# A feed-forward block by seven products: two more blocks of this form, one weight sum moved into an accumulating DMA, and another way to merge two streams of work

## The chip, the cores and the metric

The kernel runs on one core of a Trainium2 chip. The metric is the device time of one execution in microseconds (us). TensorE (PE) multiplies, VectorE (DVE) and ScalarE (ACT) do elementwise work, GpSimd (POOL) does little here but issue some transfers, SyncE (SP) issues the other transfers from HBM.

## The reference

Two decoder layers over 256 tokens of width 2048, all in float32. Each layer projects the normed input, runs a spatial gating unit beside windowed attention, projects back, and then runs the feed-forward part, which is where the change lies:

```
h2 = rms_norm(x, norm2_g[l])
x = x + (jax.nn.silu(h2 @ w_gate[l]) * (h2 @ w_up[l])) @ w_down[l]
```

`w_gate` and `w_up` are 2048 x 5632, `w_down` is 5632 x 2048. The inner width of 5632 is cut into 11 blocks of 512 columns, numbered 0 to 10.

## The kernel before

**Three matmuls for one.** Every float32 weight tile is split into a rounded high part `wh` (ScalarE, L95) and the remainder `wl` (VectorE, L96). A product is then three matmuls into the same PSUM bank: high x high, high x low, low x high (`mm3`, L124 to L127). A loaded raw tile holds 2 x 512 columns per partition (512 KB). A *standard unit* (`unit`, L129) loads one such tile, splits it and issues 12 matmuls (two row blocks, two token tiles). The raw tiles have a ring of 6 buffers, `wh` and `wl` rings of 4 each.

**Two forms of a feed-forward block.** In the standard form (`gate_up`, L651) a block takes 8 units for the gate and 8 for the up projection. In the other form (`seven`, L568) the two token tiles and the two halves of the inner dimension make a 2 x 2 by 2 x 2 block product over gate and up together, computed by seven products in the manner of Strassen and Winograd in place of eight. This needs sums of activations (made once per layer) and four sums of weight tiles per step, done by VectorE:

```
t1 = b11 + b12                     (L594)
t2 = t1 + b22                      (L595)
b12 = b12 + b22                    (L596)
kept[i] = t2 of step i, + b21      (L621, in the second half)
```

Each product is an `s_unit` (L571): split one tile, issue 6 matmuls. A block has a first half of 4 steps with 4 products each (banks m0 to m3), an evacuation of the four banks (L605 to L612), a second half of 4 steps with 3 products each (banks n0 to n2, L615 to L625), and a second evacuation with the gate (L626 to L632). So a block takes 28 products of 6 matmuls. `t1` takes a raw buffer; the four `t2` of a block live from the first half into the second in a ring of four.

**Down projection.** `down` (L665) takes two blocks at a time: for each of four column blocks it runs two units per block and adds the result to the residual (L680). It cannot start before the activations of its blocks are transposed (`act_T`, L556, some two to three units of work after the block's end, into the eight-deep ring `aT`). While they are missing, it yields False.

**Two streams.** `s_stream` (L638) runs the blocks of `S_BLOCKS` in the seven-product form. `std_stream` (L686) runs `STD_ORDER`: the remaining blocks in standard form and all down projections. The loop at L693 to L702 merges them: `s_stream` yields 0.5 after each product and "turn" at each evacuation, and the loop takes standard units according to what is owed: `STD_SHARE` (1.42) per 1.0, raised to at least 2 at a turn, in a `while`. What is still owed while down yields False stays owed. Standard units left at the end run behind the last block. The framework places instructions on each engine by its own priorities, so the order on an engine follows this program order only roughly.

Of the kernel before, what the change touches and what calls it, by code (L numbers as in the profile page):

```python
# [16 lines left out]
ALU = mybir.AluOpType  # L17
# [22 lines left out]
NI = 3584 // NB  # L40
NFF = DFF // NB
ND = D // NB
S_BLOCKS = (1, 3, 5, 7, 8, 9, 10)
STD_ORDER = (
    ("gu", 0), ("gu", 2), ("down", (0, 1)), ("gu", 4), ("down", (2, 3)), ("gu", 6),
    ("down", (4, 5)), ("down", (6, 7)), ("down", (8, 9)), ("down", (10,)),
)
STD_SHARE = 1.42
RL = 512
WARM = 12  # L50

# [12 lines left out]
def trunk(ctx, tc, x, xt, w_in, w_out, w_gate, w_up, w_down, sgu_w, sgu_g, consts,  # L64
          rel_bias, onehot, radd, out):
    nc = tc.nc
# [15 lines left out]
    def raw_load(src, parts=1):  # L82
        raw = wp.tile([P, 2, NB], F32, tag="raw", name="raw", bufs=6)
        n = 2 // parts
        for i in range(parts):
            nc.sync.dma_start(raw[:, i * n : (i + 1) * n, :], src[:, i * n : (i + 1) * n, :])
        return raw

    def split2(raw):
        wh = wp.tile([P, 2, NB], F32R, tag="wh", name="wh", bufs=4)  # L90
        wl = wp.tile([P, 2, NB], F32R, tag="wl", name="wl", bufs=4)
        step = 2 if clock[0] > 1 else 1
        for j in range(0, 2, step):
            src = raw[:, j : j + step, :]
            nc.scalar.copy(wh[:, j : j + step, :], src)  # L95
            nc.vector.tensor_tensor(  # L96
                wl[:, j : j + step, :], src, f(wh[:, j : j + step, :]), ALU.subtract
            )
        return wh, wl
# [8 lines left out]
    def tick(w=1.0):  # L108
        clock[0] += w
        due = sorted((e for e in pending if e[0] <= clock[0]), key=lambda e: e[:2])  # L110
        pending[:] = [e for e in pending if e[0] > clock[0]]
        for e in due:
            e[2]()
# [10 lines left out]
    def mm3(acc, ah, al, wh, wl, first, last):  # L124
        nc.tensor.matmul(acc, ah, wh, start=first, stop=False)  # L125
        nc.tensor.matmul(acc, ah, wl, start=False, stop=False)  # L126
        nc.tensor.matmul(acc, al, wh, start=False, stop=last)  # L127
# [128 lines left out]
    for lay in range(L):  # L256
# [307 lines left out]
        def act_later(b, sg, act_T=act_T):  # L564
            for c in range(2):
                later(2 + c, lambda c=c: act_T(b, c, sg))

        def seven(b, lay=lay, pairs2=pairs2, ext2=ext2, act_later=act_later):  # L568
            bank = [pa.tile([P, NB], F32, tag="acc", name=f"m{i}") for i in range(4)]

            def s_unit(raw, m, i, op, first, last):  # L571
                wh, wl = split2(raw)
                for j in range(2):
                    ah, al = (op(2 * i + j, h) for h in range(2))
                    mm3(bank[m], ah, al, wh[:, j, :], wl[:, j, :], first and j == 0, last and j == 1)
                tick(0.5)

            def a_op(k, t):
                return lambda p, h: pairs2[p][:, h, k, t * P : (t + 1) * P]

            def e_op(n):
                return lambda p, h: ext2[p][:, h, n, :]

            kept = []
            for i in range(4):
                b12 = raw_load(w_up[lay, b, i, 0])
                b11 = raw_load(w_gate[lay, b, i, 0])
                b22 = raw_load(w_up[lay, b, i, 1])
                t1 = wp.tile([P, 2, NB], F32, tag="raw", name="t1", bufs=6)
                t2 = ap.tile([P, 2, NB], F32, tag="spt", name="t2", bufs=4)  # L590
                first, last = i == 0, i == 3
                s_unit(b11, 0, i, a_op(0, 0), first, last)
                yield 0.5
                nc.vector.tensor_tensor(t1, b11, b12, ALU.add)  # L594
                nc.vector.tensor_tensor(t2, t1, b22, ALU.add)  # L595
                nc.vector.tensor_tensor(b12, b12, b22, ALU.add)  # L596
                s_unit(t1, 1, i, e_op(1), first, last)
                yield 0.5
                s_unit(t2, 3, i, e_op(2), first, last)
                yield 0.5  # L600
                s_unit(b12, 2, i, e_op(0), first, last)
                yield 0.5
                kept.append(t2)
            m1 = zp.tile([P, NB], F32, tag="z", name="m1")
            nc.scalar.copy(m1, bank[0])  # L605
            u1 = zp.tile([P, NB], F32, tag="z", name="u1")
            nc.vector.tensor_tensor(u1, bank[3], m1, ALU.add)
            c22 = zp.tile([P, NB], F32, tag="z", name="c22")
            c21 = zp.tile([P, NB], F32, tag="z", name="c21")
            nc.vector.tensor_tensor(c21, bank[2], u1, ALU.add)  # L610
            nc.vector.tensor_tensor(c22, bank[1], c21, ALU.add)
            nc.vector.tensor_tensor(u1, bank[1], u1, ALU.add)  # L612
            yield "turn"
            bank = [pa.tile([P, NB], F32, tag="acc", name=f"n{i}") for i in range(3)]
            for i in range(4):  # L615
                b21 = raw_load(w_gate[lay, b, i, 1])
                b22 = raw_load(w_up[lay, b, i, 1])
                first, last = i == 0, i == 3
                s_unit(b21, 0, i, a_op(1, 0), first, last)
                yield 0.5  # L620
                nc.vector.tensor_tensor(kept[i], kept[i], b21, ALU.add)  # L621
                s_unit(kept[i], 1, i, a_op(1, 1), first, last)
                yield 0.5
                s_unit(b22, 2, i, e_op(3), first, last)
                yield 0.5  # L625
            sg = [m1, c21]  # L626
            for t, m in ((0, m1), (1, c21)):
                nc.vector.tensor_tensor(m, bank[t], m, ALU.add)
                nc.scalar.activation(m, m, AF.Silu, scale=rstd2[t])
            nc.vector.tensor_tensor(u1, bank[2], u1, ALU.add)  # L630
            for t, c in ((0, u1), (1, c22)):
                nc.vector.scalar_tensor_tensor(sg[t], c, nrstd2[t], sg[t], ALU.mult, ALU.mult)  # L632
            act_later(b, sg)
            yield "turn"
# [3 lines left out]
        def s_stream(seven=seven):  # L638
            for b in S_BLOCKS:
                yield from seven(b)  # L640
# [45 lines left out]
        def std_stream(gate_up=gate_up, down=down):  # L686
            for k, (kind, what) in enumerate(STD_ORDER):
                if kind == "gu":
                    yield from gate_up(what)
                else:  # L690
                    yield from down(what, k == len(STD_ORDER) - 1)

        other = std_stream()  # L693
        owed = 0.0
        for said in s_stream():
            owed = max(owed, 2.0) if said == "turn" else owed + said * STD_SHARE
            while owed >= 1.0 and next(other, False):
                owed -= 1.0
        seven_done[0] = True
        for went in other:  # L700
            if not went:
# [89 lines left out]
```

## Time and profile before

| | |
|---|---|
| runs, median (range) | 2025.38 us (2020.27 to 2030.16) |
| the profiled execution, its own time | 2025.57 us |
| its span, first to last instruction | 2023.9 us |
| TensorE busy | 1984.0 us, 8990 instructions |
| VectorE busy | 1666.0 us, 1925 instructions |
| ScalarE busy | 1132.3 us, 1415 instructions |
| GpSimd busy | 67.5 us, 65 instructions |
| loads on SP's queue | 407.01 MB |

A row of a group of instructions gives its line, engine, operation, result and sources by the program's names, shapes and count; then busy time in us and the mean duration of one in ns; then the time in which its engine was idle just before, and what ended most of that. Matmul rows overlap: a matmul's row is longer than the distance to the next one's start. A timeline row gives start, duration, engine, line, operation, and in brackets the idle time before it with its releaser.

### The profile page before, as it was taken

To read this page: it belongs to the slowest core of one execution; us is meant where nothing else is said; L and a number is where in the kernel's file an instruction comes from. 1 tells how busy PE (TensorE), PEld (TensorE's weight loads), DVE (VectorE), ACT (ScalarE), POOL (GpSimd) and SP (SyncE) were. 2 spreads that over 40 slices of the span, in tenths; PEclk is the share of its full clock that TensorE was granted. 3 is DMA by queue.
4 is the path that set the end of the run, shared out by engine and by line. 5 is a ranking of instruction groups with operands and counts; after the bars stand their busy time and mean duration, and the time that the engine had idled before them with its cause. 6 is when DMAs were issued, how large, how long until landed. Compare 5 with 4: busy or idle time off the path is not lost.

```text
span 2023.9 us, 24694 instructions
## 1 busy us (share of the span) xinstructions
PE 1984.0 (98%) x8990; PEld 1618.5 (80%) x8990; DVE 1666.0 (82%) x1925; ACT 1132.3 (56%) x1415; POOL 67.5 (3%) x65
## 2 busy tenths in 40 slices
PE   8999999999999999999899999999999999999997
PEld 6878888888888888877687788888888888888776
DVE  5767689898989898997867776898989898989976
ACT  6455566555555555554654655666555555555543
POOL 1211000000000000000002100000000000000000
PEclk9999999999999999999999999999999999999999
DMA  9643556565766576665555344565656565657653
GB/s 323 226 162 134 187 178 227 201 235 194 238 209 234 201 236 212 234 204 193 198 188 192 131 156 179 175 233 203 239 206 234 202 239 202 233 204 241 215 186 137
DMA packets 117401, 416.02 MB, mean 206 GB/s; under 512 B 12912, under 2 KB 15088, under 8 KB 117280
## 3 DMA queue, kind: packets, MB, share of 16 engines
q1 hardware_dynamic: 115136, 407.01, 58.4%
q0 software_dynamic: 2144, 7.44, 1.2%
q8 instruction: 70, 1.15, 0.2%
q14 instruction: 51, 0.42, 0.1%
HBM read 412.27 MB, written 4.23 MB: 206 GB/s over the span
## 4 chain that ended last, share of the span: by engine, by line
PE 85%; DVE 9%; issue 2%; DMA 1%; ACT 1%; POOL 1%; SPq 0%; POOLq 0%; ACTq 0%; DVEq 0%
PE dacc L125 12%; PE dacc L126 12%; PE dacc L127 12%; PE acc L126 8%; PE acc L125 8%; PE acc L127 8%; DVE wl L96 4%; PE m L126 4%; PE m L127 4%; PE m L125 4%; PE n L126 3%; PE n L127 3%; PE n L125 3%; PE ps_v L382 1%; DMA raw<-in_w_gate_dram 1%
## 5 line engine op out<-in xcount | busy, mean ns | idle before, releaser
L95 ACT CAST wh<-raw 128x1024 fp32r<-128x1024 f32 (+1 forms) x706 | 739.5, 1050 | 593.2 <-PE dacc L127 293.2
L96 DVE TENSOR_TENSOR wl<-raw,wh 128x1024 fp32r<-128x1024 f32 (+1 forms) x706 | 853.7, 1219 | 207.9 <-ACT wh L95 198.5
L95 ACT CAST wh<-t 128x1024 fp32r<-128x1024 f32 x168 | 177.1, 1054 | 184.6 <-PE dacc L127 116.9
L125 PE MATMUL dacc<-wh,aT 128*128 128x512 f32 x640 | 251.4, 393 | 2.3 <-DVE xres L680 1.5
L127 PE MATMUL dacc<-wh,aT 128*128 128x512 f32 x640 | 250.0, 391 | 0.0
L126 PE MATMUL dacc<-wl,aT 128*128 128x512 f32 x640 | 249.9, 391 | 0.0
L96 DVE TENSOR_TENSOR wl<-t,wh 128x1024 fp32r<-128x1024 f32 x168 | 204.0, 1219 | 17.4 <-ACT wh L95 15.4
L125 PE MATMUL dacc<-wh,hT 128*128 128x512 f32 x512 | 200.3, 391 | 0.3
L126 PE MATMUL dacc<-wl,hT 128*128 128x512 f32 x512 | 199.5, 390 | 0.3 <-DVE wl L96 0.2
L127 PE MATMUL dacc<-wh,hT 128*128 128x512 f32 x512 | 199.4, 389 | 0.0
L126 PE MATMUL acc<-wl,hT 128*128 128x512 f32 x448 | 176.8, 395 | 7.8 <-DVE wl L96 7.8
L125 PE MATMUL acc<-wh,hT 128*128 128x512 f32 x448 | 180.6, 406 | 2.1 <-ACT wh L95 2.1
L127 PE MATMUL acc<-wh,hT 128*128 128x512 f32 x448 | 176.6, 394 | 0.0
L125 PEld LDWEIGHTS dacc<-wh,aT 128*128 128x128 f32 x640 | 120.1, 188 | 30.1 <-issue 3.1
L127 PEld LDWEIGHTS dacc<-wh,aT 128*128 128x128 f32 x640 | 120.7, 189 | 25.6
L126 PEld LDWEIGHTS dacc<-wl,aT 128*128 128x128 f32 x640 | 120.9, 189 | 24.5
L126 PE MATMUL m<-wl,ext 128*128 128x512 f32 x336 | 132.6, 395 | 4.6 <-DVE wl L96 4.6
L125 PE MATMUL m<-wh,ext 128*128 128x512 f32 x336 | 132.7, 395 | 1.1 <-ACT wh L95 1.1
L127 PE MATMUL m<-wh,ext 128*128 128x512 f32 x336 | 132.1, 393 | 0.0
L125 PE MATMUL acc<-wh,aT 128*128 128x512 f32 x320 | 127.8, 399 | 0.7 <-ACT aT L560 0.7
L126 PE MATMUL acc<-wl,aT 128*128 128x512 f32 x320 | 125.3, 392 | 0.0
L127 PE MATMUL acc<-wh,aT 128*128 128x512 f32 x320 | 124.1, 391 | 0.0
(157 smaller groups left out, 2980.7 us busy)
## 6 DMA issues: line engine op xcount, KB each, us to landing
raw<-in_w_up_dram SPq DMA_DIRECT2D x232, 512.0 KB, 4.3
raw<-in_w_gate_dram SPq DMA_DIRECT2D x176, 512.0 KB, 4.1
raw<-in_w_down_dram SPq DMA_DIRECT2D x176, 512.0 KB, 4.1
raw<-in_w_in_dram SPq DMA_DIRECT2D x108, 512.0 KB, 4.2
raw<-in_w_out_dram SPq DMA_DIRECT2D x64, 512.0 KB, 3.2
bias<-rdram POOLq DMA_DIRECT2D x8, 512.0 KB, 5.6
xr<-in_xt_dram SPq DMA_DIRECT2D x8, 256.0 KB, 6.0
raw<-in_w_in_dram SPq DMA_DIRECT2D x8, 256.0 KB, 5.8
```

The lines of the kernel that those rows point to most:

```text
L95: nc.scalar.copy(wh[:, j : j + step, :], src)
L96: nc.vector.tensor_tensor(wl[:, j : j + step, :], src, f(wh[:, j : j + step, :]), ALU.subtract)
L125: nc.tensor.matmul(acc, ah, wh, start=first, stop=False)
L126: nc.tensor.matmul(acc, ah, wl, start=False, stop=False)
L127: nc.tensor.matmul(acc, al, wh, start=False, stop=last)
L382: nc.tensor.matmul(pv[:, i, :], pt[:, i * nkb + b, :], zkv[b][:, (NKV + g) * HD : (NKV + g + 1) * HD], start=b == 0, stop=b == nkb - 1,)
```

## The change

Nine blocks in place of seven take the seven-product form (2 to 10; 0 and 1 stay standard). The order of the standard stream is rewritten for that. `STD_SHARE` goes from 1.42 to 0.83. The fourth weight sum (L621) leaves VectorE: right after the product that uses `t2`, a DMA on GpSimd's queue reads the `w_gate` tile from HBM once more and adds it into `t2` in place; `b21` itself is still loaded for its own product. The merge loop takes at most one standard unit after a product and up to two at a turn; a unit taken at a turn is paid back out of the following ones, as what is owed may now become negative.

```diff
-S_BLOCKS = (1, 3, 5, 7, 8, 9, 10)
+S_BLOCKS = (2, 3, 4, 5, 6, 7, 8, 9, 10)
 STD_ORDER = (
-    ("gu", 0), ("gu", 2), ("down", (0, 1)), ("gu", 4), ("down", (2, 3)), ("gu", 6),
-    ("down", (4, 5)), ("down", (6, 7)), ("down", (8, 9)), ("down", (10,)),
+    ("gu", 0), ("down", (0, 2)), ("gu", 1), ("down", (1, 3)), ("down", (4, 5)),
+    ("down", (6, 7)), ("down", (8, 9)), ("down", (10,)),
 )
-STD_SHARE = 1.42
+STD_SHARE = 0.83
...
                 s_unit(t2, 3, i, e_op(2), first, last)
+                nc.gpsimd.dma_start(t2, w_gate[lay, b, i, 1], accum_op=ALU.add)
                 yield 0.5
...
                 s_unit(b21, 0, i, a_op(1, 0), first, last)
                 yield 0.5
-                nc.vector.tensor_tensor(kept[i], kept[i], b21, ALU.add)
                 s_unit(kept[i], 1, i, a_op(1, 1), first, last)
...
         for said in s_stream():
-            owed = max(owed, 2.0) if said == "turn" else owed + said * STD_SHARE
-            while owed >= 1.0 and next(other, False):
-                owed -= 1.0
+            turn = said == "turn"
+            owed += 0.0 if turn else said * STD_SHARE
+            for k in range(2):
+                if (turn or (k == 0 and owed >= 1.0)) and next(other, False):
+                    owed -= 1.0
```

## The prediction

> **What bounds the kernel now.** The page first: one execution, TensorE (PE) busy for nearly all of the span, VectorE (DVE) next.
>
> ```profile
> span 2023.9 us, 24694 instructions
> ...
> PE 1984.0 (98%) x8990; PEld 1618.5 (80%) x8990; DVE 1666.0 (82%) x1925; ACT 1132.3 (56%) x1415; POOL 67.5 (3%) x65
> ...
> q1 hardware_dynamic: 115136, 407.01, 58.4%
> ```
>
> Shares are averages over stages, so the windows come next: length, busy time and instruction count of PE, PEld, DVE, ACT and POOL, then granted clock, DMA share, GB/s. Six rows lie in layer 0, where the feed-forward part starts at about 300 us; the one from 1892 is the same place one layer later.
>
> ```profile
> 350.00:500.00 150.00, 150.00 (x675) 124.22 (x674) 129.64 (x125) 85.72 (x88) 0.00 (x0) 1.00 0.64 217
> 500.00:650.00 150.00, 149.84 (x671) 123.38 (x670) 134.95 (x130) 84.32 (x86) 0.00 (x0) 1.00 0.65 219
> 650.00:800.00 150.00, 149.80 (x667) 123.21 (x666) 128.03 (x123) 83.47 (x85) 0.00 (x0) 1.00 0.67 226
> 876.00:886.00 10.00, 10.00 (x45) 8.28 (x45) 10.00 (x10) 7.57 (x8) 0.00 (x0) 1.00 0.63 210
> 886.00:996.00 110.00, 98.35 (x409) 76.50 (x408) 89.84 (x90) 54.46 (x57) 0.00 (x0) 0.97 0.58 201
> 1892.00:2002.00 110.00, 99.52 (x409) 77.66 (x409) 89.55 (x90) 54.37 (x57) 0.00 (x0) 0.95 0.56 191
> ...
> 966.00:976.00 10.00, 7.33 (x25) 4.52 (x25) 10.00 (x12) 4.17 (x5) 0.00 (x0) 0.95 0.42 150
> ```
>
> While standard units lie between the products, PE never pauses and sets the pace; DVE follows at 85 to 90%. Near the end of each layer the cover runs out: DVE is full and PE starves. A matmul's row overlaps the next one's, so the pitch comes from the timeline (start, duration):
>
> ```profile
> 873.11 0.39 PE L126 MATMUL n<-wl,hT 128*128 128x512 f32 x1
> 873.34 0.39 PE L127 MATMUL n<-wh,hT 128*128 128x512 f32 x1
> 873.56 0.39 PE L125 MATMUL n<-wh,hT 128*128 128x512 f32 x1
> ...
> 869.50 1.22 DVE L96 TENSOR_TENSOR wl<-t,wh 128x1024 fp32r<-128x1024 f32 x1
> 870.63 1.22 DVE L621 TENSOR_TENSOR t<-t,raw 128x1024 f32<-128x1024 f32 x1
> 871.77 1.22 DVE L96 TENSOR_TENSOR wl<-raw,wh 128x1024 fp32r<-128x1024 f32 x1
> ```
>
> Matmuls start 0.227 us apart: a product unit of 6 takes PE 1.36 us, a standard unit of 12 takes 2.72. Back to back, DVE's 1.22 us instruction costs 1.134, that is 0.085 less than its row. I take 0.085 off the 512-wide rows too: 0.60 for a tensor_tensor, 0.66 for L632 (an estimate).
>
> ```profile
> L95 ACT CAST wh<-raw 128x1024 fp32r<-128x1024 f32 (+1 forms) x706 | 739.5, 1050 | 593.2 <-PE dacc L127 293.2
> L96 DVE TENSOR_TENSOR wl<-raw,wh 128x1024 fp32r<-128x1024 f32 (+1 forms) x706 | 853.7, 1219 | 207.9 <-ACT wh L95 198.5
> ...
> L594 DVE TENSOR_TENSOR t<-raw 128x1024 f32<-128x1024 f32 x56 | 68.4, 1222 | 1.0
> L621 DVE TENSOR_TENSOR t<-t,raw 128x1024 f32<-128x1024 f32 x56 | 68.0, 1220 | 16.4 <-DMA raw<-in_w_gate_dram 16.4
> ...
> L680 DVE TENSOR_TENSOR xres<-dacc,xres 128x512 f32<-128x512 f32 x80 | 51.6, 681 | 0.5 <-PE dacc L127 0.3
> L561 DVE TENSOR_TENSOR aT<-ps_f,aT 128x512 fp32r<-128x512 f32 x44 | 29.9, 683 | 0.1
> L632 DVE SCALAR_TENSOR_TENSOR m<-u,nr,m 128x512 f32<-128x512 f32 x14 | 10.4, 743 | 0.0
> L607 DVE TENSOR_TENSOR u<-m,m 128x512 f32<-128x512 f32 x14 | 9.6, 684 | 0.8 <-ACT m L605 0.8
> ```
>
> **The change, part by part.** (1) Two more blocks by seven products. A block costs PE 28 x 6 = 168 matmuls in place of 16 x 12 = 192. Two blocks, two layers: 96 matmuls fewer, 96 x 0.227 = **-21.8 us**, on PE's own path.
>
> On DVE such a block adds 12 splits and 12 sums (24 x 1.134 = 27.2) and nine evacuations (7 x 0.60 + 2 x 0.66 = 5.5) in place of two (1.3): +31.4, so +62.8 per layer. (2) The fourth sum goes: 28 x 1.134 = -31.8 per layer. Net +31. Adding up a layer's feed-forward part (units, sums, evacuations, L680, L561) gives DVE about 609 us before and 640 after, against PE's 692 and 681. ACT gains 24 casts of 1.05 us and stays under two thirds. On average PE still binds; the question is the order.
>
> (3) The even merge. I counted units by following the two generators yield by yield. Before, in the last blocks the down stream waits for activations: the second halves of blocks 9 and 10 run with no standard unit between products. After, the last three blocks have cover throughout and 14 standard units remain behind them. In the rows 886 to 996 and 1892 to 2002 stand 409 instructions, 16 of them transposes at about 0.15 us (eight stand between 891.55 and 893.10 below, with one matmul). Full pace would need 393 x 0.227 + 2.4 = 91.6 of the 110 us: 18.4 us lost in each layer, slow-clock matmuls included. I take back 17 in each, as some waits at group ends remain: **-34 us**; the other end is 37.
>
> (4) New stalls. In an even merge a first half (16 products, 12 sums) carries more DVE work than PE work. For block 8, with 7 standard units: PE 16 x 1.36 + 7 x 2.72 + 0.6 = 41.3; DVE 35 x 1.134 + 2.4 (bank evacuation) + 2.4 (L680) + 0.6 = 45.1. Second halves run the other way (30.5 against 24.2), so DVE can regain 6. Positive differences add up to 36 us per layer, 7.8 of them in block 3. The worst stretch is the start: both units of the turn, then seven products with no cover (PE 16.1, DVE 15 x 1.134 + 3.1 + 1.2 = 21.3): 5.2 us. What lead can DVE have? The trace has the case:
>
> ```profile
> 862.88 1.06 ACT L95 CAST wh<-raw 128x1024 fp32r<-128x1024 f32 x1 [1.67 <-PE dacc L127]
> ...
> 889.88 0.39 PE L125 MATMUL m<-wh,ext 128*128 128x512 f32 x1
> 891.55 0.41 PE L189 MATMUL ps_f<-ident,m 128*128 128x128 f32 x2 [1.28 <-DVE m L632]
> ...
> 892.83 0.27 PE L189 MATMUL ps_f<-ident,c 128*128 128x128 f32 x1
> 894.39 0.50 PE L126 MATMUL m<-wl,ext 128*128 128x512 f32 x1 [1.28 <-DVE wl L96]
> ```
>
> At 862.88 ACT waits for PE, so the split buffers are full. From the middle of block 9 to block 10's second product DVE had 2.4 + 14 x 1.134 + 1.2 + 4 x 1.134 + 3.1 + 5 x 1.134 = 32.8 us of work, PE 2 x 2.72 + 13 x 1.36 + 1.2 = 24.3. PE ran dry for only 890.11 to 894.39 less 1.55 us of work, 2.7 us. So a lead of 8.5 - 2.7 = 5.8 us was absorbed, a little over the 5.2 needed. I take 0.75 us of stall for each of the eight covered blocks, near the end at zero; the other end is their whole 28 us per layer.
>
> Block 3 is not covered: down waits for block 0's activation, so its first half gets three standard units (7.8 - 5.8 = 2 us) and its turn gets none. The uncovered turn of before cost 10 - 25 x 0.227 = 4.3 us in the window from 966, and some 0.7 of slow clock behind it (matmuls 0.42 us apart in place of 0.227); 3.4 of it are three sums that will no longer be there:
>
> ```profile
> 970.07 3.48 DVE L621 TENSOR_TENSOR t<-t,raw 128x1024 f32<-128x1024 f32 x3
> ...
> 975.54 0.63 PE L125 MATMUL n<-wh,hT 128*128 128x512 f32 x1
> 975.96 0.63 PE L126 MATMUL n<-wl,hT 128*128 128x512 f32 x1
> ```
>
> That leaves 1.6 to 5.0; I take 3. New stalls: 8 x 0.75 + 2 + 3 = 11 per layer, **+22 us**.
>
> (5) The accumulating DMA, an operation that this trace does not show. The nearest rows are the plain loads, on SP's and on GpSimd's queue (KB each, us to landing), and GpSimd's issue:
>
> ```profile
> raw<-in_w_up_dram SPq DMA_DIRECT2D x232, 512.0 KB, 4.3
> ...
> bias<-rdram POOLq DMA_DIRECT2D x8, 512.0 KB, 5.6
> ```
> ```profile
> L325 POOL DMA_DIRECT2D bias<-rdram x8: 788/804/823, 46.9 to 1124.2; - x8
> ```
>
> It is issued behind t2's split and read by kept[i]'s. The shortest way between them (i = 3) holds 11 products and some three standard units, 23 us of PE; 5.6 us to land is hidden, and so is a landing three times as long. GpSimd is idle there, and 36 x 0.8 us of issues hold nobody up: behind a waiting issue stand only later sums. Were one late, every later cast would stand behind kept[i]'s on ACT, and PE after them. SP's queue has 300 loads per layer in place of 292; that six raw buffers feed products without cover is seen at 876, where DVE is full. Per block PE needs 28 x 1.36 + 11.6 x 2.72 = 69.7 us; in that time come 31.6 plain loads and 4 accumulating ones. Now 219 GB/s fill 0.65 of the queues, so full is about 337 GB/s, 44.8 loads in 69.7 us: an accumulating one may cost 3.3 plain ones before transfers bind. I cost it at 0; the ends are 0 and case C below. The Trainium skill says (Collectives: The Full Stack, "The bandwidth ceiling: the fold count and why AG ≠ RS ≠ AR") that an add inside the DMA is slow not for its arithmetic but because it reads two sources. By it the price would be two loads, DMA would be 0.88 full and the sum the same; by it case C would not occur; no trace here shows it yet. (6) By my count block 6's activation pairs meet eight live ones in an eight-deep ring. They are needed more than a block later, so the work that goes around hides it: 0.
>
> **Sum.** 2023.9 - 21.8 - 34 + 22 = 1990 for the span; the profiled execution took 2025.57, 1.7 more, hence **1992 us**. It lay 0.2 us from the median of the runs, 2025.38; nothing is corrected for that.
>
> **Rivals.** A: the lead covers everything; only the 1.6 of the bare turn and the larger recovery remain: 2023.9 - 21.8 - 37 + 3 + 2 = 1970. For it: the second halves have room. Against: sums wait for loads (L621's 16.4 us).
>
> B, the slower side: DVE sets the pace of the first halves. If its lead is not rebuilt, every surplus is paid: 2 x 36 + 2 x 3 = 78 in place of 22, so 2048. It decides from 56 us, 3.1 per block, on. For it: DVE at 10.00 of 10.00 at 876. Against: the 5.8 us shown.
>
> C: the accumulating DMA is slow. At four plain loads each a block needs 47.6 loads, 74.1 us in place of 69.7: 18 x 4.4 = +79, 2071. For it: nothing here shows its price; against: a factor over 3.3 is much.
>
> D: DVE keeps GpSimd from writing descriptors. DVE runs 20 us without a gap near 866 to 886; a sum that only then starts lands 25.6 us after its issue, 2.6 behind its 23 us: 18 x 2.6 = 47, 2039. Against: the issues take 788 to 823 ns at all places, early and late. The Trainium skill warns of this very trap (SBUF — State Buffer, "SBUF: two separate sides"), but for instructions in a two-port mode. By it these two-input sums would be spared, and L96's 1.219 us for 1024 elements shows no doubled rate: the trace agrees as far as it goes.
>
> E: the merge does not cover the ends: 2023.9 - 21.8 + 22 + 2 = 2026.
>
> **Chances.** Forecast 0.54 (its own range 1977 to 2018), A 0.15, B 0.16, C 0.08, D 0.03, E 0.04. The range goes from A to B, 1968 to 2050. No change means within 0.5%, 2015 to 2035.5, about what this measurement can tell. Faster: most of the forecast (0.50) and A, 0.65. Same: 0.04 of the forecast, E, and 0.04 of B where part of the surplus is absorbed, 0.12. Slower: the rest of B, C and D, 0.23.
>
> **What would show it.** Right: about 96 fewer matmuls of 512 columns, L621 gone, PE at 10.0 of 10 in the last blocks, DVE at 92 to 96% in the merged part, one short hole per layer in block 3. Wrong: PE waiting for L96 in every first half (B); casts waiting for raw loads, landings over 8 us (C); casts of t2 waiting for GpSimd's queue (D); matmuls at the slow pitch of 0.42 us outside block 3.

## The result and the profile after

| | median of the runs (us) | ratio to the kernel before, 95% interval |
|---|---|---|
| kernel before, in the same batch | 2023.85 (4 runs) | 1 |
| changed kernel | 2053.11 (2048.43 to 2059.41, 4 runs) | 1.0143 [1.0102, 1.0184] |

The change made the kernel 1.4% slower; 1992 us, 1.6% faster, had been forecast. The profiled execution of the changed kernel took 2059.41 us, the longest of the four runs. The page of the changed kernel, with span, busy time by engine, the two large DMA queues (packets, MB, share of 16 engines' time) and the shares of the chain that ended last:

```profile
span 2057.7 us, 24971 instructions
...
PE 1987.9 (97%) x8894; PEld 1599.6 (78%) x8894; DVE 1727.0 (84%) x1993; ACT 1175.8 (57%) x1467; POOL 129.4 (6%) x137
...
q1 hardware_dynamic: 117440, 415.40, 57.7%
q0 software_dynamic: 12512, 45.19, 11.9%
...
PE 62%; DVE 24%; DMA 5%; issue 5%; ACT 3%; POOL 1%; SPq 0%; ACTq 0%; DVEq 0%; POOLq 0%
```

The counts are as forecast: 8990 - 8894 = 96 matmuls fewer, and VectorE (DVE) is busy 61 us longer (2 x 31 had been worked out). Yet 96 fewer matmuls took 3.9 us more of busy time, and the span grew by 33.8. The shares look harmless: TensorE (PE) 97% busy, DVE 84%. The chain tells more: DVE holds 24% of it, where it held 9% before.

The windows, cut at the first evacuation of each block of layer 0 (L613, whose line ends the fence with first and last start). Columns as before: length, busy time and count of PE, PEld, DVE, ACT, POOL, granted clock, DMA share, GB/s.

```profile
345.00:416.00 71.00, 68.97 (x300) 55.36 (x298) 64.12 (x63) 45.18 (x49) 3.38 (x4) 0.98 0.76 237
416.00:499.00 83.00, 78.89 (x342) 62.87 (x343) 74.85 (x75) 45.29 (x46) 3.41 (x4) 1.00 0.79 249
499.00:574.00 75.00, 73.36 (x318) 59.71 (x317) 68.77 (x66) 45.19 (x47) 3.41 (x4) 0.98 0.80 250
574.00:650.00 76.00, 71.10 (x307) 56.60 (x306) 67.66 (x66) 43.69 (x46) 3.40 (x4) 0.98 0.77 246
650.00:727.00 77.00, 74.83 (x329) 60.41 (x328) 70.56 (x71) 44.91 (x46) 3.40 (x4) 1.00 0.75 235
727.00:800.00 73.00, 70.55 (x310) 56.80 (x308) 69.79 (x68) 44.14 (x45) 3.41 (x4) 1.00 0.81 247
800.00:879.00 79.00, 75.35 (x326) 60.11 (x327) 72.02 (x71) 44.61 (x46) 3.41 (x4) 1.00 0.79 250
879.00:956.00 77.00, 73.78 (x320) 58.57 (x319) 70.91 (x70) 44.21 (x45) 3.41 (x4) 1.00 0.77 250
...
L613 DVE TENSOR_TENSOR u<-m,u x9: 677/677/684, 345.0 to 955.6; 128x512 f32<-128x512 f32 x9
```

Busy time hides the loss here (a matmul that starts after a pause has a longer row); the count shows it. In the rows from 345 and 574 us 16 of PE's instructions are transposes, in the others 8; these start 0.11 us apart, and the rest need 0.227 us each. So the first row holds 284 x 0.227 + 1.8 = 66.3 us of work and lost 4.7; the eight rows lost 4.7, 6.3, 3.7, 8.1, 3.2, 3.5, 5.9 and 5.3. An instruction that lies across a cut counts in both rows, so the eight blocks are better taken in one piece, here in layer 0 and in layer 1:

```profile
345.00:956.00 611.00, 586.83 (x2542) 470.43 (x2541) 558.68 (x543) 357.22 (x367) 27.22 (x32) 0.99 0.78 246
1365.40:1981.40 616.00, 592.37 (x2541) 473.50 (x2541) 558.52 (x542) 355.94 (x367) 27.10 (x32) 0.98 0.77 244
```

Each holds 80 transposes, so some 568 us of work: **43 us are lost in layer 0 and 48 in layer 1, 5 to 6 per block**, in every block and not in block 3 alone. In the kernel before PE never paused between 350 and 800 us (x667 to x675 in 150 us). The two make 92; by the forecast's own sum, 2057.7 - (2023.9 - 21.8 - 34) = **89.6 us**, where 22 stood.

The loss lies in the first halves. Cut at each block's first L632 as well, the eight second halves of layer 0 last 238.6 us and hold 1051 matmuls, which is 238.6 us of work; the eight first halves last 372.1 us and hold 334 us of work (both to some 3 us, for the instructions across the cuts). Block 9, first half and second half:

```profile
829.10:878.58 49.48, 46.19 (x200) 36.21 (x200) 48.09 (x48) 26.86 (x28) 3.41 (x4) 1.00 0.84 249
878.58:906.80 28.22, 28.22 (x127) 23.36 (x126) 23.88 (x25) 17.49 (x18) 0.00 (x0) 1.00 0.71 249
```

What the engines waited for (engine, line, for what: us in total, times, longest) in the changed kernel:

```profile
ACT wh L95 <- DVE t L594: 109.8, 44, 4.8
...
ACT wh L95 <- DVE t L595: 42.8, 35, 3.1
...
PEld m L125 <- ACT wh L95: 37.0, 47, 1.7
...
ACT wh L95 <- DMA raw<-in_w_down_dram: 34.8, 16, 4.7
...
PE m L125 <- ACT wh L95: 19.9, 35, 1.4
```

and in the kernel before:

```profile
ACT wh L95 <- DVE t L594: 20.8, 6, 4.0
```

PE waits above all in the products of the first halves (banks m), for the high part of a split; ScalarE (ACT), which makes it, waits for the sums t1 and t2. The first half of block 9, which has standard units around it, shows how. Its windows of 4 us:

```profile
836.00:840.00 4.00, 4.00 (x23) 3.39 (x22) 4.00 (x5) 3.09 (x5) 0.84 (x1) 1.00 0.48 171
840.00:844.00 4.00, 3.86 (x17) 2.84 (x16) 3.97 (x5) 1.16 (x2) 0.00 (x0) 1.00 0.92 189
844.00:848.00 4.00, 2.45 (x8) 1.60 (x9) 4.00 (x5) 3.22 (x4) 0.00 (x0) 1.00 0.85 333
848.00:852.00 4.00, 4.00 (x19) 3.29 (x19) 4.00 (x5) 1.97 (x2) 0.86 (x1) 1.00 0.93 207
...
856.00:860.00 4.00, 3.63 (x16) 2.69 (x15) 4.00 (x4) 3.06 (x3) 0.33 (x1) 1.00 0.86 263
...
864.00:868.00 4.00, 3.06 (x14) 2.25 (x13) 3.45 (x3) 2.54 (x3) 0.00 (x0) 1.00 1.02 375
868.00:872.00 4.00, 3.70 (x17) 2.72 (x16) 3.82 (x4) 3.00 (x4) 0.86 (x1) 1.00 1.00 327
```

DVE has hardly a gap; PE keeps pace for some 15 us out of the filled split buffers, runs dry at 844 and again at 856 and 864. The timeline of the first hole (start, duration, engine; in brackets the idle time and its releaser), ahead of it two casts of the second half before, from 446 us:

```profile
446.71 1.06 ACT L95 CAST wh<-raw 128x1024 fp32r<-128x1024 f32 x1 [0.31 <-PE n L127]
448.07 1.05 ACT L95 CAST wh<-raw 128x1024 fp32r<-128x1024 f32 x1 [0.30 <-PE n L127]
...
841.93 1.21 DVE L594 TENSOR_TENSOR t<-raw 128x1024 f32<-128x1024 f32 x1
843.17 1.23 DVE L595 TENSOR_TENSOR t<-t,raw 128x1024 f32<-128x1024 f32 x1
844.32 1.22 DVE L596 TENSOR_TENSOR raw<-raw 128x1024 f32<-128x1024 f32 x1
...
843.23 1.05 ACT L95 CAST wh<-t 128x1024 fp32r<-128x1024 f32 x1 [2.84 <-DVE t L594]
...
844.33 0.50 PE L125 MATMUL m<-wh,ext 128*128 128x512 f32 x1 [0.47 <-ACT wh L95]
845.61 0.50 PE L125 MATMUL m<-wh,ext 128*128 128x512 f32 x1 [0.78 <-ACT wh L95]
```

In a second half ACT waits for PE: the four split buffers are full, and no more lead can be stored. In a first half its longest waits are for DVE's sums, and PE goes on when ACT's cast is done, 1.2 us after the sum's end (843.14 to 844.33).

### The profile page after: what moved, and what is told of

Read it like the earlier page. It is cut to its first block, busy times and chain, and to the rows that moved or that the text cites. A ratio compares the mean times of both kernels' runs of the same rounds, so it can differ in the third digit from the quotient of the medians.

```text
span 2057.7 us, 24971 instructions
## 1 busy us (share of the span) xinstructions
PE 1987.9 (97%) x8894; PEld 1599.6 (78%) x8894; DVE 1727.0 (84%) x1993; ACT 1175.8 (57%) x1467; POOL 129.4 (6%) x137
## 3 DMA queue, kind: packets, MB, share of 16 engines
q1 hardware_dynamic: 117440, 415.40, 57.7%
q0 software_dynamic: 12512, 45.19, 11.9%
q8 instruction: 70, 1.15, 0.2%
## 4 chain that ended last, share of the span: by engine, by line
PE 62%; DVE 24%; DMA 5%; issue 5%; ACT 3%; POOL 1%; SPq 0%; ACTq 0%; DVEq 0%; POOLq 0%
DVE wl L96 12%; PE acc L126 8%; PE acc L127 8%; PE acc L125 8%; PE dacc L126 6%; PE dacc L127 6%; PE dacc L125 5%; PE n L127 3%; PE n L126 3%; PE n L125 3%; ACT wh L95 3%; DVE t L595 3%; DMA raw<-in_w_down_dram 2%; PE m L126 2%; PE m L127 2%
## 5 line engine op out<-in xcount | busy, mean ns | idle before, releaser
L95 ACT CAST wh<-raw 128x1024 fp32r<-128x1024 f32 (+1 forms) x706 | 736.4, 1049 | 532.0 <-PE acc L127 174.8
L96 DVE TENSOR_TENSOR wl<-raw,wh 128x1024 fp32r<-128x1024 f32 (+1 forms) x706 | 850.9, 1219 | 195.3 <-ACT wh L95 181.7
L95 ACT CAST wh<-t 128x1024 fp32r<-128x1024 f32 x216 | 227.3, 1053 | 211.6 <-DVE t L594 109.8
L96 DVE TENSOR_TENSOR wl<-t,wh 128x1024 fp32r<-128x1024 f32 x216 | 259.7, 1218 | 20.2 <-ACT wh L95 15.6
L125 PE MATMUL dacc<-wh,aT 128*128 128x512 f32 x608 | 235.8, 395 | 12.9 <-ACT wh L95 10.2
L127 PE MATMUL dacc<-wh,aT 128*128 128x512 f32 x608 | 237.6, 391 | 0.0
L125 PE MATMUL m<-wh,ext 128*128 128x512 f32 x432 | 176.6, 412 | 20.3 <-ACT wh L95 19.9
L126 PE MATMUL m<-wl,ext 128*128 128x512 f32 x432 | 175.5, 406 | 9.5 <-DVE wl L96 9.3
L127 PE MATMUL acc<-wh,hT 128*128 128x512 f32 x448 | 175.8, 392 | 0.0
L127 PE MATMUL m<-wh,ext 128*128 128x512 f32 x432 | 174.2, 403 | 0.0
L600 POOL DMA_DIRECT2D t<-in_w_gate_dram x72 | 61.3, 852 | 1402.9 <-DVE wl L96 1197.7
L125 PEld LDWEIGHTS dacc<-wh,aT 128*128 128x128 f32 x608 | 112.9, 188 | 45.9 <-ACT wh L95 19.4
L125 PE MATMUL acc<-wh,aT 128*128 128x512 f32 x352 | 139.1, 395 | 0.0
L127 PE MATMUL acc<-wh,aT 128*128 128x512 f32 x352 | 137.5, 391 | 0.0
L127 PEld LDWEIGHTS dacc<-wh,aT 128*128 128x128 f32 x608 | 114.7, 189 | 24.1
L125 PEld LDWEIGHTS m<-wh,ext 128*128 128x128 f32 x432 | 82.9, 192 | 51.0 <-ACT wh L95 35.2
L125 PE MATMUL n<-wh,hT 128*128 128x512 f32 x288 | 112.5, 391 | 1.8 <-ACT wh L95 1.8
```

What stands on the lines that cost most here:

```text
L96: nc.vector.tensor_tensor(wl[:, j : j + step, :], src, f(wh[:, j : j + step, :]), ALU.subtract)
L600: nc.gpsimd.dma_start(t2, w_gate[lay, b, i, 1], accum_op=ALU.add)
```

## The experiments

Two theories stood against each other. **Theory S**, as the expectations call it: DVE sets the pace of the first halves, because the second halves cannot store its spare time (rival B of the prediction). Against it: the accumulating DMA delays the raw loads (theory T of the expectations), or the new order of blocks leaves holes. The runs of one group share their runs of the kernel before; a difference between ratios of two groups carries both intervals.

### Which sum costs: three edits of the changed kernel

```diff
-                nc.gpsimd.dma_start(t2, w_gate[lay, b, i, 1], accum_op=ALU.add)
```

> The changed kernel without the accumulating DMA: t2 is used again as it is, so w_gate's second half is left out of the fourth weight sum. VectorE's work stays the same, 72 transfers of 512 KB fall away. Theory S (VectorE's surplus of work in the first halves, which its lead does not cover): the DMA costs nothing, 2045 to 2058 us. Theory T (the accumulating transfers make the raw loads late): most of the loss goes, 2000 to 2025 us.

```diff
-                nc.gpsimd.dma_start(t2, w_gate[lay, b, i, 1], accum_op=ALU.add)
...
+                nc.vector.tensor_tensor(kept[i], kept[i], b21, ALU.add)
```

> The changed kernel with the fourth sum back on VectorE in the second halves (36 more instructions of 1.134 us per layer, 4.5 us per block, where VectorE has about 6 us of room) and no accumulating DMA. Theory S: VectorE can rebuild less lead, 2055 to 2085 us. Theory T: as without the DMA, 2000 to 2035 us.

```diff
-                nc.vector.tensor_tensor(b12, b12, b22, ALU.add)
+                nc.vector.tensor_tensor(b12[:, :, :32], b12[:, :, :32], b22[:, :, :32], ALU.add)
```

> The changed kernel with the third sum of each step (L596, b12 + b22) made over 64 of its 1024 columns; the rest of b12 is used without b22. VectorE has about 1.0 us less per step, 36 per layer, all in the first halves; transfers and order stay. Theory S: the surplus of a covered first half (about 4 us) is gone, only the uncovered blocks 3 and 6 still stall: 1985 to 2010 us. Theory T: 2040 us or more.

| run | median us | ratio, interval |
|---|---|---|
| e1_no_sum4 | 2046.79 | 1.0095 [1.0078, 1.0112] |
| e2_sum4_dve | 2061.76 | 1.0171 [1.0153, 1.0190] |
| e3_thin_sum3 | 2013.12 | 0.9925 [0.9906, 0.9944] |

Without the DMA the loss stays: the waits for L594 in e1 are 109.8 us, as with it. Two rows of the grouped instructions, the fourth sum in e2 and the thin third sum in e3:

```profile
L621 DVE TENSOR_TENSOR t<-t,raw 128x1024 f32<-128x1024 f32 x72 | 86.3, 1219 | 4.5 <-DMA raw<-in_w_gate_dram 4.5
```
```profile
L596 DVE TENSOR_TENSOR raw<-raw 128x64 f32<-128x64 f32 x72 | 15.7, 218 | 0.0
```

e3 takes 72 us of DVE's time out of the first halves, and 46 come off the span (2057.7 to 2011.7); its time lies 3 us above the range that S had for it. e2 puts 86 us of DVE's time into the second halves, and against e1 the time grows by 0.76%, 15 us. It is the place of DVE's work that counts, not its sum: this speaks for S and against the average of the prediction's step (2). ACT's waits by themselves are no measure of the loss: in e3 it still waits 86.2 us for L594, while the weight loads of the products in banks m wait 17.5 us for L95 in place of 37.0.

### The parts of the change without the two blocks

Both start from the kernel before, with its seven blocks and its order.

```diff
+                nc.gpsimd.dma_start(t2, w_gate[lay, b, i, 1], accum_op=ALU.add)
...
-                nc.vector.tensor_tensor(kept[i], kept[i], b21, ALU.add)
```

> The kernel before with one part of the change: the fourth sum by the accumulating DMA, seven blocks and the old merge kept. Theory S: VectorE had room there, so only the bare ends gain (three sums of 1.134 us in the last turn, some in block 9): 2008 to 2022 us. Theory T: the 56 added transfers cost time here too: 2030 us or more.

The second has this edit and the merge loop of the change:

```diff
-            owed = max(owed, 2.0) if said == "turn" else owed + said * STD_SHARE
-            while owed >= 1.0 and next(other, False):
-                owed -= 1.0
+            turn = said == "turn"
+            owed += 0.0 if turn else said * STD_SHARE
+            for k in range(2):
+                if (turn or (k == 0 and owed >= 1.0)) and next(other, False):
+                    owed -= 1.0
```

> The kernel before with two parts of the change: the accumulating DMA and the new merge loop, but seven blocks, the old order of the standard stream and STD_SHARE 1.42. Counted unit by unit, every half then has more PE work than VectorE work (sum of surpluses 0), and the ends are covered. Theory S: the end stalls of 17 to 18 us per layer go, 1980 to 1995 us. If instead the merge loop itself does the harm: above 2015 us.

e4: 2012.19 us, 0.9924 [0.9904, 0.9945]. Its span is 2008.5 us, 15.4 shorter, and the gain lies in the uncovered ends: the windows 886 to 996 and 1892 to 2002 hold 438 and 448 instructions in place of 409 each, 68 x 0.227 = 15.4 us. e5, with the merge added: **1990.20 us, 0.9809 [0.9792, 0.9826]**, the fastest of the kernels that compute the whole. Its page and the window of its last blocks:

```profile
span 1988.0 us, 24835 instructions
...
876.00:986.00 110.00, 109.14 (x487) 89.73 (x485) 89.33 (x89) 59.48 (x62) 2.56 (x3) 1.00 0.76 248
```

Before, 409 instructions stood in such 110 us. The DMA and the even merge together cover the ends: 2023.9 - 1988.0 = 36 us, where the prediction's step (3) had 34; 15 of them come with the DMA, which takes the fourth sum off DVE, and 21 with the merge. From e5 to the changed kernel only the two blocks, the order and the share are left: 0.9809 to 1.0143, all of the loss and more.

### Order of the blocks, place of the standard units, size of the lead

```diff
-    ("gu", 0), ("down", (0, 2)), ("gu", 1), ("down", (1, 3)), ("down", (4, 5)),
-    ("down", (6, 7)), ("down", (8, 9)), ("down", (10,)),
+    ("gu", 0), ("down", (2,)), ("gu", 1), ("down", (0, 3)), ("down", (1, 4)), ("down", (5, 6)),
+    ("down", (7, 8)), ("down", (9,)), ("down", (10,)),
```

> The changed kernel with another STD_ORDER (block 0, down of 2, block 1, down of 0 and 3, 1 and 4, 5 and 6, 7 and 8, 9, 10), by which no down projection finds its activations missing, so blocks 3 and 6 have cover too. Surplus of the first halves 29.7 us per layer in place of 36.3, and no bare turn. Theory S: about 10 us per layer less, 2028 to 2040 us. If the bare stretches in blocks 3 and 6 are the main harm: below 2015 us.

The next has this order too, and puts the standard units, which need more PE time than DVE time, where DVE is short; the yields of 0.0 are the three of the second halves:

```diff
-STD_SHARE = 0.83
+STD_SHARE = 0.95
...
-                yield 0.5
+                yield 0.0
...
-            turn = said == "turn"
-            owed += 0.0 if turn else said * STD_SHARE
-            for k in range(2):
-                if (turn or (k == 0 and owed >= 1.0)) and next(other, False):
+            if said == "turn":
+                for k in range(2):
+                    next(other, False)
+            else:
+                owed += said * STD_SHARE
+                if owed >= 1.0 and next(other, False):
                     owed -= 1.0
```

> As e6_order, but the same number of standard units lies elsewhere: two at each turn, not paid back, the rest behind products of the first halves only (STD_SHARE 0.95 there, 0 in the second halves). PE and VectorE work then agree in every half (surplus 1.7 us per layer in all). Theory S: the stalls go but for jitter, 1980 to 2005 us. If mean load or transfers were the cause, placing the same units elsewhere changes little: above 2025 us.

The third edits the changed kernel alone:

```diff
-        wh = wp.tile([P, 2, NB], F32R, tag="wh", name="wh", bufs=4)
-        wl = wp.tile([P, 2, NB], F32R, tag="wl", name="wl", bufs=4)
+        wh = wp.tile([P, 2, NB], F32R, tag="wh", name="wh", bufs=3)
+        wl = wp.tile([P, 2, NB], F32R, tag="wl", name="wl", bufs=3)
```

> The changed kernel with rings of three in place of four for wh and wl, so ScalarE and VectorE can be one unit less ahead of PE. If the lead absorbs part of each first half's surplus: one unit (1.36 to 2.72 us) less in most of 36 halves, 2070 to 2110 us. If no lead is ever built up there: within 10 us of the changed kernel's 2053 us.

| run | median us | ratio, interval |
|---|---|---|
| e6_order | 2040.35 | 1.0055 [1.0034, 1.0075] |
| e7_cover_first | 2016.41 | 0.9926 [0.9901, 0.9950] |
| e8_lead3 | 2111.88 | 1.0413 [1.0398, 1.0429] |

The order without missing activations is worth 0.9%, the place of the standard units another 1.3%, with the same instructions on every engine as in e6. But S had expected 1980 to 2005 us of e7, where DVE's work was to fit in every half by count, and its runs took 2005 to 2018. e7's waits show what else comes late:

```profile
ACT wh L95 <- DVE t L594: 83.2, 45, 3.8
ACT wh L95 <- DMA raw<-in_w_down_dram: 80.8, 38, 4.5
```

e8 takes away one of the four split buffers. Its L613 rows lie further apart:

```profile
L613 DVE TENSOR_TENSOR u<-m,u x9: 679/681/683, 356.4 to 984.5; 128x512 f32<-128x512 f32 x9
```

That is 628.1 us for eight blocks against 610.6, 2.2 per block or 1.1 per half. So a lead exists and is used (the time lies 2 us above the range for that), and a buffer of it is worth a little less than one product unit of 1.36 us; another 11 us of what e8 loses lie ahead of layer 0's first evacuation (356.4 against 345.0).

### What is left when cover comes first

Three edits of e7_cover_first: without the DMA (e9, as e1), with the thin third sum (e10, as e3), with both (e12).

> e7_cover_first without the accumulating DMA; t2 is used again as it is, without w_gate's second half. VectorE's work and the order stay. What is left in e7 over the 1990 us of e5 is 26 us. If it is late raw loads (casts wait 80.8 us for w_down loads there): 1990 to 2002 us. If it is VectorE, busy at 95% in every stretch: 2008 to 2018 us.

> e7_cover_first with the third sum over 64 of 1024 columns, b12 otherwise without b22: VectorE has 36 us less per layer, transfers stay. If the rest in e7 is VectorE: 1975 to 1995 us. If it is late loads: 2008 us or more.

> e7_cover_first with both reliefs at once: no accumulating DMA (t2 without w_gate's second half) and the third sum over 64 of 1024 columns. If late loads and VectorE are what is left between e7 (2016 us) and the time that PE's instructions alone need (e5's 1990 us less 96 matmuls of 0.227 us, 1968 us): 1968 to 1985 us, that is the two single gains of 16 and 19 us added. If a third cause stands behind them: 1990 us or more.

| run | median us | ratio, interval |
|---|---|---|
| e9_cover_nodma | 1996.99 | 0.9841 [0.9819, 0.9863] |
| e10_cover_thin | 2000.35 | 0.9859 [0.9840, 0.9877] |
| e12_cover_floor | 1971.91 | 0.9720 [0.9704, 0.9736] |

One wait of e9, with the same name as above:

```profile
ACT wh L95 <- DMA raw<-in_w_down_dram: 33.7, 22, 2.3
```

and the windows of e12, which may be set against the changed kernel's:

```profile
350.00:500.00 150.00, 148.55 (x663) 121.54 (x662) 137.91 (x142) 94.83 (x98) 0.00 (x0) 1.00 0.71 232
500.00:650.00 150.00, 149.30 (x671) 123.28 (x669) 138.89 (x142) 94.56 (x98) 0.00 (x0) 1.00 0.70 232
...
L612 DVE TENSOR_TENSOR u<-m,u x9: 676/678/680, 345.5 to 916.6; 128x512 f32<-128x512 f32 x9
```

Without the DMA ACT's waits for w_down's tiles fall from 80.8 to 33.7 us. e9 lies in the range that was given for late loads; e10 lies between its two ranges, so DVE's work is part of what e7 has left, and not all of it. Together the two edits bring 44.5 us, more than their 19.4 and 16.1; why the last 9 come only with both is open. In e12 the weight loads of banks m wait 1.1 us for L95. With both, the blocks stand 71.4 us apart in place of 76.3, and PE's path is what the prediction worked out: 2023.9 - 21.8 - 34 = 1968 against a span of 1973.2.

### Eight blocks, from e7_cover_first

```diff
-S_BLOCKS = (2, 3, 4, 5, 6, 7, 8, 9, 10)
+S_BLOCKS = (2, 4, 5, 6, 7, 8, 9, 10)
-    ("gu", 0), ("down", (2,)), ("gu", 1), ("down", (0, 3)), ("down", (1, 4)), ("down", (5, 6)),
-    ("down", (7, 8)), ("down", (9,)), ("down", (10,)),
+    ("gu", 0), ("down", (2,)), ("gu", 1), ("down", (0, 4)), ("gu", 3), ("down", (1, 5)),
+    ("down", (3, 6)), ("down", (7, 8)), ("down", (9,)), ("down", (10,)),
-STD_SHARE = 0.95
+STD_SHARE = 1.2
...
-                yield 0.0
+                yield 0.1
```

> Eight blocks by seven products (2, 4 to 10) with the accumulating DMA, the cover placed as in e7 (STD_SHARE 1.2, little of it behind second halves) and an order without waits. By count no half has more VectorE than PE work; PE has 48 matmuls (10.9 us) fewer than e5. Theory S: 1978 to 1992 us, as fast as e5 or faster. If eight blocks already cost VectorE too much: above 2000 us.

1996.55 us, 0.9841 [0.9818, 0.9863]: 0.85% faster than nine blocks in e7, not faster than the seven of e5, and above the 1978 to 1992 that S had for it. So the count of work per half, by which no half had too much for DVE, does not foretell the time to 1%. One more block (-10.9 us of PE work) pays for itself at best.

## Why the prediction was wrong

**(1) Matmuls saved: right.** 96 fewer, and e12 shows their 21.8 us once nothing else is late.

**(2) DVE's load: right in size, and the wrong thing to ask.** DVE's busy time grew by 61 us. "On average PE still binds" holds for a layer; within a first half it does not.

**(3) The even merge: the size is right, for both parts together.** e5 brings 36 us with DMA and merge, where 34 were forecast; the merge's share of them is 21. The 15 of the DMA come from sums that left DVE in the ends, which the step did not set apart.

**(4) New stalls: this step failed.** It put 0.75 us on a covered block, on the ground that a lead of 5.8 us absorbs the worst stretch of 5.2, and 22 us in all; 89.6 were lost. (The top of its own range, 2018, does not follow from it: the whole 28 us per layer give 2036, and the measured time lies above that too.) Four things were wrong in it:

- The lead was too large and the worst stretch too short. How far DVE is ahead can be read directly, from the end of a split to the matmul that uses it. In the kernel before, at the place from which 5.8 was read:

```profile
862.91 1.22 DVE L96 TENSOR_TENSOR wl<-raw,wh 128x1024 fp32r<-128x1024 f32 x1
866.99 0.39 PE L126 MATMUL dacc<-wl,aT 128*128 128x512 f32 x1
```

In the changed kernel, at the start of block 9's first half and at its last hole:

```profile
824.99 1.23 DVE L96 TENSOR_TENSOR wl<-raw,wh 128x1024 fp32r<-128x1024 f32 x1 [0.29 <-ACT wh L95]
828.01 0.39 PE L126 MATMUL dacc<-wl,aT 128*128 128x512 f32 x1
...
869.46 0.50 PE L126 MATMUL dacc<-wl,aT 128*128 128x512 f32 x1 [0.30 <-DVE wl L96]
```

The split was done 2.9 us ahead before (864.13 to 866.99), and 1.8 us ahead here (826.22 to 828.01). With its four buffers full ACT waits for PE (the 0.30 us waits "<-PE n L127"), and DVE's further spare time is lost; here three product units came last, and four buffers of those hold less of PE's time than with standard units among them (1.36 against 2.72 us each). The 5.8 had counted from where DVE begins a stretch, its evacuation and first split included. From 827.79 to the last hole at 869.46 PE had 157 matmuls and 8 transposes, 36.5 of 41.7 us: 5.2 us were lost on top of the lead of 1.8. So DVE was some 7 us short up to there, where the step had 5.2 for its worst stretch and 3.8 for a whole half: the shortage does not end with the first seven products, it grows until the last sums of the half are made (866.3 us). This working is for one half; the other first halves of layer 0 lose 2.6 to 8.4 us by the same cuts as above. What is paid is thus near the surplus that rival B had priced, 78 us, 2048; with some 10 for the DMA (below) it gives 88 of the 89.6. So close an agreement is partly luck, since B's sum holds none of the next three points.
- The surplus was a little too small. DVE's 1.134 us per instruction does not hold for a sum that reads the sum just before it: from 841.93 to 843.17 are 1.24 us. So it is in 34 of the 72 pairs of L594 and L595, 4 us over both layers; in the others something else stands between the two.
- Block 3 was said to be the one bare block. Block 6 is bare too: the pair (1, 3) waits for block 1's activations. The row 574 to 650, which holds block 6's first half, lost 8.1 us, the most of all; the row with block 3's first half, 345 to 416, lost 4.7, no more than a covered one. The order that avoids both (e6) is worth 0.9%.
- The slow clock was counted for the bare turn alone, and it comes with the holes of other halves. From 540 to 550 us, in block 5's first half and right behind three holes, the granted clock was 0.83 and matmuls stood 0.43 us apart:

```profile
540.00:550.00 10.00, 9.28 (x34) 7.42 (x34) 9.28 (x9) 4.37 (x5) 0.86 (x1) 0.83 0.86 247
```

By windows of 10 us some 5 us of layer 0 and 10 of layer 1 went this way (an estimate from their granted clocks). The mean clock was 0.991, against 0.994 before and 0.997 in e3 and e12, which have fewer holes.

**(5) The accumulating DMA: the price was right, the cost of 0 was not.** Rows of the changed kernel, GpSimd's issue (min/median/max ns) and the landing:

```profile
L600 POOL DMA_DIRECT2D t<-in_w_gate_dram x72: 832/850/941, 299.2 to 1972.2; - x72
...
raw<-in_w_down_dram SPq DMA_DIRECT2D x176, 512.0 KB, 4.8
...
t<-in_w_gate_dram POOLq DMA_DIRECT2D x72, 512.0 KB, 7.0
```

It lands in 7.0 us (23 were to be had), and no cast is seen waiting for it. On q0 it took 11.9% less 1.2% (what e1, without it, has there) of 16 x 2057.7 us: 48.9 engine-us for each of 72, against 57.7% x 16 x 2057.7 / 792 = 24.0 for a plain load. That is 2.04 loads, under the 3.3 from which transfers would bind on the mean. The Trainium skill's rule of two source reads (Collectives: The Full Stack, "The bandwidth ceiling: the fold count and why AG ≠ RS ≠ AR") says two, and the trace agrees. But the mean was again the wrong measure: the queues are full in stretches (1.02 and 1.00 at 864 to 872), and casts wait 34.8 us for w_down's raw tiles, against 12.5 in e1 and 3.7 in the kernel before. The DMA costs 0.5% in the changed kernel (e1; the two intervals together reach from 0 to 0.9%), 0.85% in e7 and 1.4% where the sums no longer hold things up (e10 to e12). Each limit hides part of the other.

**(6) The aT ring** was not tried by itself. It is seen: ACT's casts into it wait 9.5 us for the down projections' matmuls, four times, at 701 and 710 us and one layer later, where block 6's pairs are made; before, they never did. No harm shows: the row 650 to 727, which holds two of these waits, lost 3.2 us, the least of all, and e5, the fastest, has 7.6 us of them.

**The rivals.** B is what happened, in kind. A's 1970 is reached only without third sum and DMA (e12). C needed four loads; it was 2.04. D: the issues take 850 ns with DVE full, 804 before, and nothing waited for them; the Trainium skill's warning (SBUF — State Buffer, "SBUF: two separate sides") had spared these sums, and the trace agrees. E is ruled out by e5, and by the 467 instructions of the changed kernel from 886 to 996 us, where 409 stood. Of the signs named beforehand, "PE waiting for L96 in every first half" came true, with the wait mostly on L95, one step ahead of it. So did the slow pitch outside block 3, and, in part, the sign of C: casts waited for raw loads, and the accumulating load took up to 9.5 us to land.

**The account.** From the changed kernel to e12's 0.972 there are 4.2%: order 0.9, place of the cover 1.3, DMA 0.85, third sum 1.2 in this sequence of runs; another sequence would share them otherwise. What was gained and given back: DMA -0.8% (e4) and merge -1.15% (e5) were real; the two blocks with their order and share took 3.3% back.

## What to carry to other kernels

When one engine's work comes in phases, compare the loads phase by phase; here DVE's mean of 91% (558.7 of 611 us) beside PE's 96% did not show who set the pace, since the ring of four buffers carried only 2 to 3 us from a phase with slack to one without. Put the filler work of the bounding engine where the other engine is short, not evenly. Before trading matmuls for sums, ask which engine makes the sums at that moment: here a block saved 10.9 us of PE, and the two together cost more than they saved, while the two plain parts of the change were worth 1.9% alone.

## What the runs showed of the hardware that was not expected

A sum on DVE that reads the result of the one just before starts 1.24 to 1.26 us after it (34 pairs); with a split between them the second starts 1.13 to 1.14 behind that. An accumulating 512 KB load costs the DMA engines 2.04 plain loads to within the reading of the queue's shares and lands 2.2 us later (7.0 against 4.8). A transfer for which no cast was seen waiting still cost 0.5 to 1.4%, most likely through the loads beside it, with the DMA engines 0.80 busy in e7's window from 350 to 500 us and 0.71 in e9's, without it.
